# A two-layer decoder trunk on one core: PE queue order at the entry and the transition, and a later place for each chunk's finish

## The chip, the cores and the metric

The kernel runs on one NeuronCore of one Trainium2 chip. The core has five engines with queues of their own: PE (TensorE, matrix products), DVE (VectorE), ACT (ScalarE), POOL (GpSimd) and SP (SyncE, which here issues all transfers). Each engine works through its queue in the order in which the program was laid down, and waits at an instruction until its inputs are there. The metric is the device time of one execution in microseconds.

## What is computed

A decoder trunk on one sequence of 1024 tokens with 1024 channels, in float32: a short-convolution layer (A), then an attention layer (B) with 16 heads, then a root-mean-square norm.

```
# layer A
h = rmsnorm(x, g) * (1 + scale) + shift          # shift, scale, gate from silu(c) @ w + b
b_gate, c_gate, u, z = split(h @ w_in, 4)
y = b_gate * causal_dwconv(c_gate * u, conv_w) * silu(z)
x = x + gate * (y @ w_out)
# layer B
k, v = split(modulated_norm(x) @ w_kv, 2);  q, z = split(modulated_norm(x) @ w_qz, 2)
per 128-query block: s = q k^T / 8;  lb = log_sigmoid(s);  l1 = where(mask, lb - s, 0)
suffix = reversed_cumsum(l1) - l1;  a = where(mask, exp(lb + suffix), 0);  o = a v
x = x + gate * ((o * silu(z)) @ w_out)
out = rmsnorm(x, final_g)
```

## The kernel before, in words

All activations are kept transposed: 128 channels on the partitions, tokens along the columns, so a 1024x1024 activation is eight tiles of 128x1024. Every float32 operand of a product is split into a high part and a remainder (`xh`/`xl`, `whi`/`wlo`), and a product is three matmuls: high by high, high by rest, rest by high. The function `linear` (L181) does that for one output tile: 8 channel tiles times 3 matmuls, 24 in all, into one PSUM bank of 512 tokens (a "half"; NH is 2). A PSUM bank is named by its tag: `ps_mm`, `ps_z`, `ps_tr` and `ps_o`, two banks each; `ps_any` hands out the first three in turn.

The order on the engines is set by a scheduler that takes the instructions in program order as priority, fills gaps with later work by its own timing estimate, and obeys two extra means: `tc.high_priority()` and `tc.issue_after(i)`, which keeps the instructions of a block on the engine of `i` behind `i`.

The norms are all made the same way. The squares of eight channel tiles are summed into one tile; PE sums it over the partitions (`column_totals`, L105, or transposes and a reduction, L91 and L92); DVE makes 1/sqrt of the few numbers in twelve small steps (`rms_columns`, L202 to L209, the result is `ry`); PE spreads `ry` over all partitions by transposes (`row_block`, L215); and the result is multiplied into the tiles.

Entry of layer A (L305 to L324): the first tiles of the four projections of layer A (M_B, M_C, M_U, M_Z) are multiplied with the raw, not yet normalised `xh`/`xl` by `lin`, while the modulation vectors and the norm are still on their way. `spread = last["pe"]` is the last transpose that spreads the norm.

Transition (L430 to L475, L566 to L573): the output projection of layer A gives x1 half by half, eight tiles `s` each. For a half, L448 to L453 make the scale, L455 scales the eight tiles on DVE, L456 and L457 split them into `x1h` and `x1l`. Three weight tiles of layer B (`firsts`: a key, a query and a value tile) are prepared early; each has a vector `terms` whose sum over channels is the bias of its projection. `with_bias` (L493) makes that bias when it is first used: `shift_bias` (L174) transposes `terms` on PE (L177) into `ps_mm` and reduces it on DVE (L178). Then `project_qkv(0)` makes keys, queries and values of pair 0 for both halves; ACT and DVE add the bias as they read the bank (L521, L522).

The end (L766 to L778): the last output projection runs over three chunks of tokens, 512, 256 and 256 wide. For each chunk the tiles j = 4 to 7 are multiplied (24 matmuls each; tiles 0 to 3 were done before), then squared. A chunk's `finish` (L750) makes its norm and multiplies its eight tiles, six on POOL and two on DVE (L754), and stores each; `finish_last` (L757) does that for the last chunk on DVE alone, reading the scale from PSUM (L763).

Of the kernel before, what the change touches and what calls it, by code (L numbers as in the profile page):

```python
# [11 lines left out]
AF = mybir.ActivationFunctionType  # L12
ALU = mybir.AluOpType
AX = mybir.AxisListType.X

P = 128
# [10 lines left out]
EARLY = 4  # L27
# [3 lines left out]
CHUNKS = ((0, 512), (512, 768), (768, 1024))  # L31
# [6 lines left out]
def decoder_kernel(ctx, tc, vecs, xT, a_mod, kv_mod, b_mod, w_in, w_out_a, w_kv, w_qz, w_out_b, outT):  # L38
    nc = tc.nc
# [10 lines left out]
    last = {}  # L50
# [120 lines left out]
                acc, raw[:, kt * P:(kt + 1) * P], shift[:, kt:kt + 1], acc, op0=ALU.mult, op1=ALU.add)  # L171
        return acc

    def shift_bias(acc, tag):  # L174
        bias = const.tile([P, 1], F32, name="bias", tag="bias", bufs=8)
        ps = ps_tile(tag)
        nc.tensor.transpose(ps[:, :P], acc, ident)  # L177
        nc.vector.tensor_reduce(bias, ps[:, :P], AX, ALU.add)  # L178
        return bias

    def linear(ps, w, ah, al, sl, kts=range(KT)):  # L181
        hi, lo = w
        for kt in kts:
            wh, wl = hi[:, kt * P:(kt + 1) * P], lo[:, kt * P:(kt + 1) * P]
            nc.tensor.matmul(ps, lhsT=wh, rhs=ah[kt][:, sl], start=(kt == kts[0]), stop=False)  # L185
            nc.tensor.matmul(ps, lhsT=wh, rhs=al[kt][:, sl], start=False, stop=False)  # L186
            nc.tensor.matmul(ps, lhsT=wl, rhs=ah[kt][:, sl], start=False, stop=(kt == kts[-1]))  # L187


    def rms_columns(ssq, lo_t=0, hi_t=T, more=None, total=None):  # L190
# [36 lines left out]
    def halves():  # L227
        return [slice(h * HALF, (h + 1) * HALF) for h in range(NH)]
# [13 lines left out]
    M_B, M_C, M_U, M_Z = 0, 1, 2, 3  # L242
# [59 lines left out]
            split(hi_b, lo_b, raw_b, nc.gpsimd)  # L302
            first[M_B] = raw_b, hi_b, lo_b

    def lin(w):  # L305
        out = []
        for sl in halves():
            ps = ps_any()
            linear(ps, w, xh, xl, sl)
            out.append(ps)  # L310
        return out

# [8 lines left out]
        rms_rows(y_a, rbc_a)  # L321
    spread = last["pe"]

    first[M_B] = first[M_B][0], lin(first[M_B][1:])  # L324


    def modulated(x, gain, rms, shift, hi, lo):
# [104 lines left out]
    for sl in halves():  # L432
        ssq1 = tmp.tile([P, HALF], F32, name="ssq1", tag="graw", bufs=3)
        xs = []
        for j in range(KT):
            w = load_weights(w_out_a[j])[1:]
            xr = stile()
            xs.append(xr)
            nc.sync.dma_start(xr, xT[j * P:(j + 1) * P, sl])
            ps = ps_any()  # L440
            linear(ps, w, yh, yl, sl)
            nc.vector.scalar_tensor_tensor(xr, ps, mods["gate_a"][:, j:j + 1], xr, op0=ALU.mult, op1=ALU.add)
            nc.sync.dma_start(x1_dram[j, :, sl], xr)
            if j == 0:
                nc.scalar.activation(ssq1, xr, AF.Square)
            else:
                sq = tmp.tile([P, HALF], F32, name="sq1", tag="graw", bufs=3)
                nc.scalar.activation(sq, xr, AF.Square)  # L448
                if j < KT - 1:
                    nc.vector.tensor_add(ssq1, ssq1, sq)  # L450
        with tc.high_priority():

            scale = row_block(rms_columns(ssq1, 0, HALF, sq), 0, 4)  # L453
            for kt, x in enumerate(xs):
                nc.vector.tensor_mul(x, x, scale)  # L455
                nc.scalar.activation(x1h[kt][:, sl], x, AF.Copy)  # L456
                last["x1"] = nc.vector.tensor_tensor(x1l[kt][:, sl], x, x1h[kt][:, sl].bitcast(F32), op=ALU.subtract)  # L457
        if sl.start == 0:

            def first_raw(raw, w, m):  # L460
                nc.sync.dma_start(raw, w)
                return raw, scaled(raw, mods["gain_" + m], mods["shift_" + m])

            firsts = [
                first_raw(tmp.tile([P, D], F32, name="raw1", tag="gacc", bufs=1), w_kv[0], "kv"),
                first_raw(tmp.tile([P, 2 + T], F32, name="raw1", tag="v", bufs=2)[:, :T], w_qz[0], "b"),
                first_raw(raw_tile(), w_kv[NPAIR], "kv")]

    def parts(raw, pool=wpool, tags=("whi", "wlo"), bufs=2):
        hi, lo = (pool.tile([P, KT * P], F32R, name=n, tag=t, bufs=bufs) for n, t in zip(("whi", "wlo"), tags))  # L470
        split(hi, lo, raw, nc.gpsimd)
        return hi, lo

    first_w = [parts(raw) for raw, _ in firsts[:2]]
    papw.close()  # L475

# [17 lines left out]
    def with_bias(w, terms):  # L494
        bias = []

        def late():

            if not bias:
                bias.append(shift_bias(terms, "mm"))  # L500
            return bias[0]
        return w, late

    def projected(w, sl, ps_get=lambda: ps_tile("mm")):
        ps = ps_get()
        linear(ps, w, x1h, x1l, sl)
        return ps
# [4 lines left out]
    def project_qkv(p):  # L512
# [26 lines left out]
        def queries(sl, t, bias):  # L539
            ql = att.tile([P, HALF], F32, name="ql", tag="pt", bufs=2).bitcast(F32R)  # L540
            evacuate(t, bias, qq[0][:, sl], ql)
            move(qq[1][B, sl], qq[0][B, sl])
            move(qq[1][A, sl], ql[B])
            move(qq[0][B, sl], ql[A])
# [21 lines left out]

        if p == 0:
            first_w.append(parts(firsts[2][0], att, ("vv", "vv"), 4))
            (kw, kb), (qw, qb), (vw, vb) = (with_bias(w, terms) for w, (_, terms) in zip(first_w, firsts))
            for sl in halves():  # L570
                keys(sl, projected(kw, sl, ps_any), kb)
                queries(sl, projected(qw, sl, ps_any), qb)
                values(sl, projected(vw, sl, ps_any), vb)  # L573
        else:
            kw, kb = prepared(w_kv[p], mods["gain_kv"], mods["shift_kv"])
            for sl in halves():
                keys(sl, projected(kw, sl), kb)
            qw, qb = prepared(w_qz[p], mods["gain_b"], mods["shift_b"])
            for sl in halves():
                queries(sl, projected(qw, sl), qb)  # L580
            vw, vb = prepared(w_kv[NPAIR + p], mods["gain_kv"], mods["shift_kv"])
            for sl in halves():
                values(sl, projected(vw, sl), vb)
# [113 lines left out]
    def add_out(x2, j, sl, w, kts):  # L697
        ps = ps_any()[:, :sl.stop - sl.start]
        linear(ps, w, oh, ol, sl, kts)
        nc.vector.scalar_tensor_tensor(x2[:, sl], ps, mods["gate_b"][:, j:j + 1], x2[:, sl], op0=ALU.mult, op1=ALU.add)  # L700
# [66 lines left out]
    for c, (a, b) in enumerate(CHUNKS):  # L767
        sl = slice(a, b)
        for j in range(EARLY, KT):
            if c == 0:  # L770
                ws[j] = load_weights(w_out_b[j], None, "vv", "vv", att, 4)[1:] if j >= KT - 2 else load_weights(w_out_b[j])[1:]
                x2.append(residual(j))
            add_out(x2[j], j, sl, ws[j], range(KT))
            sq = squares(j, sl, c == len(CHUNKS) - 1 and j == KT - 1)
        if c < len(CHUNKS) - 1:
            finish(sl)
        else:
            finish_last(sl, sq)  # L778


# [39 lines left out]
```

## Time and profile before

| | before |
|---|---|
| time, median of 3 runs | 1195.78 us (1192.18 to 1450.73) |
| the profiled execution, time | 1193.45 us |
| its span | 1191.6 us |
| PE busy | 1160.2 us, 97% of the span, 6004 matmuls |
| DVE, ACT, POOL busy | 857.4, 457.6, 351.7 us |
| mean granted TensorE clock | 0.982 of full |
| transfers | 138.47 MB, mean 116 GB/s |

A busy share is an average over stages that have different limits. Matmuls are pipelined: the time from one start to the next is what each costs, and the duration shown is longer. The granted clock has two levels, 1.00 (2.4 GHz) and 0.50 (1.2 GHz).

### The profile page before, as it was taken

The page shows a single profiled execution, that of the slowest core. Times are in us where ns is not written, and L with a number is a line of the kernel's source. Part 1 is how long each engine was busy: PE and PEld are TensorE (multiplying, and loading weights), DVE is VectorE, ACT ScalarE, POOL GpSimd, SP SyncE. Part 2 cuts the span into 40 slices and gives each one's busy share as a digit, 9 for nine tenths or more (in the row PEclk, how much of TensorE's full clock was granted, in tenths as well). Part 3 has the DMA queues.
Part 4 walks back from the last instruction along what each step waited for, and adds up shares of the span by engine and source line. Part 5 has one row for each costly group of instructions (what it writes and reads, how often), then busy time and mean ns, then how long its engine had stood idle before and what let it go on. Part 6 is the DMA issues. An engine that isn't in the chain of part 4 may idle for free.

```text
span 1191.6 us, 15883 instructions
## 1 busy us (share of the span) xinstructions
PE 1160.2 (97%) x6004; PEld 987.6 (83%) x6004; DVE 857.4 (72%) x1271; ACT 457.6 (38%) x750; POOL 351.7 (30%) x205
## 2 busy tenths in 40 slices
PE   7999999999999999989999999999999999999995
PEld 6888888888888888868888888888888888887885
DVE  7679325446546487478898898888988888686466
ACT  4344211212212224234544545444545444454341
POOL 3014423433433453321231322303123032121424
PEclk9799999999999999989999999999999999999997
DMA  9534315345354544342313223132241323562204
GB/s 373 220 123 144 104 54 165 109 151 176 99 167 150 193 141 154 114 100 70 86 65 89 63 78 99 64 85 67 63 107 53 84 67 79 143 248 88 71 1 141
DMA packets 61436, 138.47 MB, mean 116 GB/s; under 512 B 7472, under 2 KB 11696, under 8 KB 61360
## 3 DMA queue, kind: packets, MB, share of 16 engines
q1 hardware_dynamic: 61360, 137.46, 36.5%
q8 instruction: 47, 0.77, 0.3%
q14 instruction: 29, 0.24, 0.1%
HBM read 103.87 MB, written 14.68 MB: 99 GB/s over the span
## 4 chain that ended last, share of the span: by engine, by line
PE 86%; DVE 10%; issue 2%; ACT 1%; DMA 0%; DVEq 0%; SPq 0%; ACTq 0%
PE ps_mm L185 12%; PE ps_mm L186 12%; PE ps_mm L187 12%; PE ps_z L186 5%; PE ps_z L187 5%; PE ps_z L185 5%; PE ps_tr L186 5%; PE ps_tr L187 5%; PE ps_tr L185 5%; PE ps_tr L628 4%; DVE sfx L618 3%; PE ps_o L643 3%; PE ps_o L642 2%; PE ps_z L610 2%; PE ps_z L609 2%
## 5 line engine op out<-in xcount | busy, mean ns | idle before, releaser
L144 POOL TENSOR_TENSOR wlo<-raw,whi 128x1024 fp32r<-128x1024 f32 x87 | 219.4, 2523 | 632.9 <-ACT whi L143 516.2
L618 DVE TENSOR_TENSOR_SCAN sfx<-sfx,floor 128x128 f32<-128x128 f32 (+2 forms) x192 | 226.0, 1197 | 18.2 <-ACT sfx L614 18.2
L185 PE MATMUL ps_mm<-x1h,whi 128*128 128x512 f32 x480 | 191.7, 399 | 4.1 <-DVE bias L178 4.1
L186 PE MATMUL ps_mm<-x1l,whi 128*128 128x512 f32 x480 | 190.1, 396 | 0.0
L187 PE MATMUL ps_mm<-x1h,wlo 128*128 128x512 f32 x480 | 188.8, 393 | 0.0
L143 ACT ACTIVATE whi<-raw 128x1024 fp32r<-128x1024 f32 x87 | 92.1, 1059 | 144.1 <-issue 39.6
L631 ACT ACTIVATE ah<-ps_tr,minus 128x512 fp32r<-128x512 f32 (+1 forms) x160 | 100.4, 646 | 109.5 <-PE ps_tr L628 107.9
L632 DVE SCALAR_TENSOR_TENSOR al<-ps_tr,ah 128x512 fp32r<-128x512 f32 (+1 forms) x160 | 97.6, 623 | 41.7 <-ACT ah L631 41.2
L614 ACT ACTIVATE sfx<-ps_z 128x128 f32<-128x128 f32 (+2 forms) x192 | 90.4, 492 | 77.9 <-PE ps_z L610 76.2
L185 PEld LDWEIGHTS ps_mm<-x1h,whi 128*128 128x128 f32 x480 | 90.6, 189 | 22.2 <-DVE bias L178 5.1
L187 PEld LDWEIGHTS ps_mm<-x1h,wlo 128*128 128x128 f32 x480 | 90.6, 189 | 17.7
L121 DVE SCALAR_TENSOR_TENSOR gacc<-graw,cs,gacc 128x512 f32<-128x512 f32 x84 | 72.5, 885 | 44.9 <-DMA graw<-b_mod 22.1
L186 PEld LDWEIGHTS ps_mm<-x1l,whi 128*128 128x128 f32 x480 | 90.6, 189 | 16.6 <-DVE x1l L457 0.3
L628 PE MATMUL ps_tr<-ident,sfx 128*128 128x128 f32 x576 | 88.1, 274 | 0.0
L643 PE MATMUL ps_o<-al,vv 128*128 128x256 f32 x320 | 82.7, 294 | 4.3 <-DVE al L632 4.3
L642 PE MATMUL ps_o<-ah,vv 128*128 128x256 f32 x320 | 86.4, 282 | 0.1
L643 PEld LDWEIGHTS ps_o<-al,vv 128*128 128x128 f32 x320 | 60.4, 189 | 11.7 <-DVE al L632 8.7
L609 PE MATMUL ps_z<-kh,qq 128*128 128x128 f32 (+1 forms) x192 | 68.9, 364 | 0.7 <-ACT sfx L614 0.7
L642 PEld LDWEIGHTS ps_o<-ah,vv 128*128 128x128 f32 x320 | 60.5, 189 | 7.3 <-ACT ah L631 0.6
L628 PEld LDWEIGHTS ps_tr<-ident,sfx 128*128 128x128 f32 x576 | 65.5, 141 | 1.0
L610 PE MATMUL ps_z<-kl,qq 128*128 128x128 f32 (+1 forms) x192 | 65.3, 349 | 0.0
L185 PE MATMUL ps_mm<-nh,whi 128*128 128x512 f32 x152 | 59.4, 391 | 0.0
(277 smaller groups left out, 2435.0 us busy)
## 6 DMA issues: line engine op xcount, KB each, us to landing
raw<-w_in SPq DMA_DIRECT2D x29, 512.0 KB, 4.2
graw<-b_mod SPq DMA_DIRECT2D x48, 256.0 KB, 3.1
stage<-a_mod SPq DMA_DIRECT2D x16, 512.0 KB, 9.8
s<-xT SPq DMA_DIRECT2D x32, 256.0 KB, 4.8
graw<-kv_mod SPq DMA_DIRECT2D x32, 256.0 KB, 3.4
raw<-w_qz SPq DMA_DIRECT2D x16, 512.0 KB, 3.9
raw<-w_out_a SPq DMA_DIRECT2D x16, 512.0 KB, 3.5
raw<-w_kv SPq DMA_DIRECT2D x16, 512.0 KB, 3.6
```

Of the source, the lines that this page charges most:

```text
L143: nc.scalar.activation(hi, full, AF.Copy)
L144: lo_eng.tensor_tensor(lo, full, hi.bitcast(F32), op=ALU.subtract)
L185: nc.tensor.matmul(ps, lhsT=wh, rhs=ah[kt][:, sl], start=(kt == kts[0]), stop=False)
L186: nc.tensor.matmul(ps, lhsT=wh, rhs=al[kt][:, sl], start=False, stop=False)
L187: nc.tensor.matmul(ps, lhsT=wl, rhs=ah[kt][:, sl], start=False, stop=(kt == kts[-1]))
L609: nc.tensor.matmul(zps[:, :w], lhsT=qq[:, qs], rhs=kh[:, c0:c0 + w], start=True, stop=False)
L618: nc.vector.tensor_tensor_scan(rev, rev, floor[:, z0:z0 + w][:, ::-1], sf[r][:, s0 + w:s0 + w + 1], op0=ALU.mult, op1=ALU.max)
L628: nc.tensor.transpose(tp[:, s * P:(s + 1) * P], rows[r][:, jb * P - c0:(jb + 1) * P - c0], ident)
L631: nc.scalar.activation(ah[:, :w], tp[:, :w], AF.Identity, bias=minus)
L632: nc.vector.scalar_tensor_tensor(al[:, :w], tp[:, :w], -1.0, ah[:, :w].bitcast(F32), op0=ALU.add, op1=ALU.subtract)
L642: nc.tensor.matmul(ops[:, cols], lhsT=vs, rhs=ah[:, rs], start=first, stop=False)
L643: nc.tensor.matmul(ops[:, cols], lhsT=vs, rhs=al[:, rs], start=False, stop=end)
```

## The change

In the entry, the second half of M_B's first product is put behind `spread` on PE. In the transition, the three biases of `firsts` are made ahead of `project_qkv`, with high priority, behind the last matmul of layer A's output projection (`out_last`): PE transposes into `ps_tr`, and ACT reads the bank with a copy that also writes the sum of each row (L179 of the change). The queries of pair 0 are put behind the last transpose of `row_block`. At the end, a chunk's `finish` is written behind the first two tiles of the next chunk.

```
-    def shift_bias(acc, tag):
+    def shift_bias(acc, tag, eng=nc.vector):
         bias = const.tile([P, 1], F32, name="bias", tag="bias", bufs=8)
         ps = ps_tile(tag)
         nc.tensor.transpose(ps[:, :P], acc, ident)
-        nc.vector.tensor_reduce(bias, ps[:, :P], AX, ALU.add)
+        if eng is nc.scalar:
+            nc.scalar.activation(acc, ps[:, :P], AF.Copy, accum_out=bias)
+        else:
+            nc.vector.tensor_reduce(bias, ps[:, :P], AX, ALU.add)
         return bias
...
-            nc.tensor.matmul(ps, lhsT=wl, rhs=ah[kt][:, sl], start=False, stop=(kt == kts[-1]))
+            last["mm"] = nc.tensor.matmul(ps, lhsT=wl, rhs=ah[kt][:, sl], start=False, stop=(kt == kts[-1]))
...
-    def lin(w):
+    def lin(w, behind=None):
         out = []
-        for sl in halves():
+        for h, sl in enumerate(halves()):
             ps = ps_any()
-            linear(ps, w, xh, xl, sl)
+            if behind is not None and h:
+
+                with tc.issue_after(behind.ins):
+                    linear(ps, w, xh, xl, sl)
+            else:
+                linear(ps, w, xh, xl, sl)
             out.append(ps)
         return out
...
-    first[M_B] = first[M_B][0], lin(first[M_B][1:])
+    first[M_B] = first[M_B][0], lin(first[M_B][1:], spread)
...
+        out_last = last["mm"]
         with tc.high_priority():
 
             scale = row_block(rms_columns(ssq1, 0, HALF, sq), 0, 4)
...
+    with tc.high_priority(), tc.issue_after(out_last.ins):
+        first_b = [shift_bias(terms, "tr", nc.scalar) for _, terms in firsts]
     first_w = [parts(raw) for raw, _ in firsts[:2]]
     papw.close()
...
             first_w.append(parts(firsts[2][0], att, ("vv", "vv"), 4))
-            (kw, kb), (qw, qb), (vw, vb) = (with_bias(w, terms) for w, (_, terms) in zip(first_w, firsts))
+            (kw, kb), (qw, qb), (vw, vb) = ((w, lambda b=b: b) for w, b in zip(first_w, first_b))
             for sl in halves():
                 keys(sl, projected(kw, sl, ps_any), kb)
-                queries(sl, projected(qw, sl, ps_any), qb)
+
+                with tc.issue_after(last["pe"].ins):
+                    q = projected(qw, sl, ps_any)
+                queries(sl, q, qb)
                 values(sl, projected(vw, sl, ps_any), vb)
...
             add_out(x2[j], j, sl, ws[j], range(KT))
+            if j == EARLY + 1 and c > 0:
+
+                finish(slice(*CHUNKS[c - 1]))
             sq = squares(j, sl, c == len(CHUNKS) - 1 and j == KT - 1)
-        if c < len(CHUNKS) - 1:
-            finish(sl)
-        else:
-            finish_last(sl, sq)
+    finish_last(sl, sq)
```

The change's lines stand a few numbers higher: L215 of before is L218, L455 and L457 are L464 and L466, L185 to L187 are L188 to L190, L754 is L768.

PE's queue in the transition, before, from the last query matmul of the first half (into `ps_z`) to the first matmuls of the second half:

```order
L187 MATMUL ps_z<-x1h,wlo 128x512
L177 MATMUL ps_mm<-ident,bacc 128x128
L215 MATMUL ps_o<-ident,ry 128x128 x4
L177 MATMUL ps_mm<-ident,bacc 128x128
L185 MATMUL ps_z<-x1h,whi 128x512
L185 MATMUL ps_mm<-x1h,whi 128x512
L186 MATMUL ps_mm<-x1l,whi 128x512
```

The same place in the change, from the last bias product on; the keys of the first half go into `ps_mm`, the queries into `ps_z`:

```order
L177 MATMUL ps_tr<-ident,bacc 128x128
L188 MATMUL ps_mm<-x1h,whi 128x512
L189 MATMUL ps_mm<-x1l,whi 128x512
L105 MATMUL ps_o<-one,sq_3703 128x1 x4
L190 MATMUL ps_mm<-x1h,wlo 128x512
L188 MATMUL ps_mm<-x1h,whi 128x512
L189 MATMUL ps_mm<-x1l,whi 128x512
L190 MATMUL ps_mm<-x1h,wlo 128x512
L218 MATMUL ps_o<-ident,ry 128x128 x4
L188 MATMUL ps_z<-x1h,whi 128x512
```

The broadcast of `ry` has moved from behind the 24 query matmuls to ahead of them, and the bias products to ahead of L105.

DVE's queue at the same place, before, from the last two steps of `ry`:

```order
L208 SCALAR_TENSOR_TENSOR rt<-rt,rv 128x4
L209 SCALAR_TENSOR_TENSOR ry<-rt,ry 128x4
L178 TENSOR_REDUCE bias<-ps_mm 128x1
L455 TENSOR_TENSOR s<-s,ps_o 128x512 x8
L178 TENSOR_REDUCE bias<-ps_mm 128x1
L457 TENSOR_TENSOR x1l<-s,x1h 128x512 x8
```

and in the change:

```order
L211 SCALAR_TENSOR_TENSOR rt<-rt,rv 128x4
L212 SCALAR_TENSOR_TENSOR ry<-rt,ry 128x4
L464 TENSOR_TENSOR s<-s,ps_o 128x512 x8
L466 TENSOR_TENSOR x1l<-s,x1h 128x512 x8
L168 TENSOR_SCALAR bacc<-raw,shift_b 128x128
```

The reductions of the biases have left DVE's queue; on ACT the sum of the first stands ahead of the last square, the other two behind it.

PE's queue at the end, before, inside the last tile of the last chunk (`ps_mm`); the first L215 belongs to the `finish` of the middle chunk, the last to `finish_last`:

```order
L186 MATMUL ps_mm<-ol,whi 128x256
L215 MATMUL ps_o<-ident,ry 128x128 x2
L187 MATMUL ps_mm<-oh,wlo 128x256
L185 MATMUL ps_mm<-oh,whi 128x256
L186 MATMUL ps_mm<-ol,whi 128x256
...
L105 MATMUL ps_o<-one,ssq_9870 128x1 x2
L105 MATMUL ps_o<-one,sq_10434 128x1 x2
L215 MATMUL ps_o<-ident,ry 128x128 x2
```

and in the change:

```order
L189 MATMUL ps_mm<-ol,whi 128x256
L190 MATMUL ps_mm<-oh,wlo 128x256
L218 MATMUL ps_o<-ident,ry 128x128 x2
L105 MATMUL ps_o<-one,ssq_9870 128x1 x2
L105 MATMUL ps_o<-one,sq_10434 128x1 x2
L218 MATMUL ps_o<-ident,ry 128x128 x2
```

The middle chunk's broadcast has moved behind the last matmul of the program.

## Rows read from the trace of the kernel before

**Rows 1.** The head of the page.

```profile
span 1191.6 us, 15883 instructions
```

**Rows 2.** Busy time by stretch: stretch, length, each engine, PEclk, DMA share, GB/s.

```profile
20.00:507.00 487.00, 487.00 (x2253) 407.43 (x2252) 280.39 (x396) 132.03 (x174) 168.77 (x81) 0.98 0.44 147
519.00:1173.90 654.90, 648.81 (x3649) 560.56 (x3648) 542.74 (x809) 307.80 (x549) 168.72 (x104) 1.00 0.30 87
```

**Rows 3.** PE's waits: what waited, for what: total us, times, longest.

```profile
PE ps_o L215 <- DVE ry L209: 5.7, 2, 3.3
PE ps_o L643 <- DVE al L632: 4.3, 8, 0.7
PE ps_mm L185 <- DVE bias L178: 4.1, 3, 3.2
```

**Rows 4.** Timeline of PE, transition: start, length, instruction, idle before and its releaser.

```profile
500.18 0.94 PE L105 MATMUL ps_o<-one,sq 128*128 128x1 f32 x8
...
501.55 0.40 PE L185 MATMUL ps_z<-x1h,whi 128*128 128x512 f32 x1
...
507.03 0.27 PE L177 MATMUL ps_mm<-ident,bacc 128*128 128x128 f32 x1
507.14 0.60 PE L215 MATMUL ps_o<-ident,ry 128*128 128x128 f32 x4
507.69 0.33 PE L177 MATMUL ps_mm<-ident,bacc 128*128 128x128 f32 x1
509.18 0.50 PE L185 MATMUL ps_z<-x1h,whi 128*128 128x512 f32 x1 [1.17 <-ACT x1h L456]
512.90 0.80 PE L185 MATMUL ps_mm<-x1h,whi 128*128 128x512 f32 x1 [3.22 <-DVE bias L178]
...
518.63 0.39 PE L186 MATMUL ps_mm<-x1l,whi 128*128 128x512 f32 x1
```

**Rows 5.** Timeline of ACT and DVE, transition.

```profile
495.19 0.63 ACT L448 ACTIVATE sq<-s 128x512 f32<-128x512 f32 x1
...
503.35 0.16 DVE L209 SCALAR_TENSOR_TENSOR ry<-rt,ry 128x4 f32<-128x4 f32 x1
...
507.78 1.88 DVE L455 TENSOR_TENSOR s<-s,ps_o 128x512 f32<-128x512 f32 x3
...
512.57 0.28 DVE L178 TENSOR_REDUCE bias<-ps_mm 128x1 f32<-128x128 f32 x1
512.77 7.12 DVE L457 TENSOR_TENSOR x1l<-s,x1h 128x512 fp32r<-128x512 f32 x8
```

**Rows 6.** Busy time by stretch, behind the transition's waits.

```profile
515.00:517.00 2.00, 2.00 (x6) 1.60 (x5) 2.00 (x3) 0.41 (x1) 1.60 (x1) 0.50 0.46 100
```

**Rows 7.** One-column products in layer A's entry, and the clock around them.

```profile
85.10 1.84 PE L363 MATMUL ps_o<-shift_a,stage 128*128 128x1 f32 x16
85.00:87.00 2.00, 2.00 (x19) 1.96 (x18) 2.00 (x4) 0.78 (x2) 0.00 (x0) 1.00 0.64 200
```

**Rows 8.** The end: PE's timeline, and a stretch behind the first wait.

```profile
1176.58 0.40 PE L215 MATMUL ps_o<-ident,ry 128*128 128x128 f32 x2 [2.40 <-DVE ry L209]
1184.64 0.66 PE L215 MATMUL ps_o<-ident,ry 128*128 128x128 f32 x2 [3.33 <-DVE ry L209]
1177.20:1178.00 0.80, 0.80 (x7) 0.80 (x5) 0.69 (x2) 0.59 (x2) 0.00 (x0) 0.51 0.00 0
```

**Rows 9.** The end: timeline of POOL and DVE.

```profile
1165.71 8.75 POOL L754 TENSOR_TENSOR x<-x,rbc 128x512 f32<-128x512 f32 x6 [26.64 <-DVE rbc L222]
1169.48 1.26 DVE L204 TENSOR_SCALAR rt<-rv 128x2 int32<-128x2 int32 x1
...
1176.28 0.16 DVE L209 SCALAR_TENSOR_TENSOR ry<-rt,ry 128x2 f32<-128x2 f32 x1
1178.15 4.56 POOL L754 TENSOR_TENSOR x<-x,rbc 128x256 f32<-128x256 f32 x6 [3.69 <-DVE rbc L222]
1182.09 0.65 DVE L205 TENSOR_SCALAR ry<-rt 128x2 int32<-128x2 int32 x1
```

## Prediction, made before the changed kernel ran

> **What bounds the kernel now.** I read the head of the page first. The profiled execution has a span of 1191.6 us [rows 1] and a time of 1193.45 us, so 1.85 us lie around the span; it stands between the median of the three runs (1195.78) and the lowest (1192.18), and every sum below starts from 1193.45. Next I asked for PE's busy time in two long stretches: from 20 to 507 us it is busy for all 487.00 us, and from 519 to 1173.9 us for 648.81 of 654.90 [rows 2]. What an edit does inside those stretches is therefore paid only if it adds or removes PE work, or opens a gap. What is left are two places, and the list of PE's waits names them: 4.1 us for `bias`, most of it in one piece in the transition into layer B, and 5.7 us for `ry`, at the end [rows 3]. The timelines of these two places carry the rest.
>
> **The transition, PE now.** The scale of layer A's second half is made in this way: sums over partitions on PE (L105), twelve small DVE steps to `ry` (L202 to L209), a transposing broadcast on PE (L215), then DVE scales eight tiles (L455), and ACT and DVE split them (L456, L457). `ry` is ready at 503.35 + 0.16 = 503.51 [rows 5], but L215 starts only at 507.14 [rows 4]: it stands in PE's queue behind 24 query matmuls, from 501.55 to 507.03, 0.228 us each [rows 4]. Then PE has little ready: it waits 1.17 us for `x1h` and 3.22 us for a bias whose reduction (L178) stands on DVE behind the eight scalings [rows 4, 5]. And after that the clock is low: it reads 0.50 (1.2 GHz) from 515 to 517 [rows 6], and the first matmul in full pace again starts at 518.63 [rows 4]. So from 507.03 to 518.63, 11.60 us, PE does two L177 (0.11 each), one L215 (507.14 to 507.69, 0.55) and 14 matmuls (3.19): 3.96 us of work. **The transition loses 7.6 us.**
>
> **The transition, changed.** Three edits act on it. The queries are put behind L215, so the broadcast stands four matmuls after L105, with the 24 of the queries behind it. The three bias products stand earlier, and their sums move from DVE to ACT. So DVE has nothing between the last step of `ry` and the eight scalings. Step by step: ahead of L105 there are two matmuls less (0.46) and two L177 more (0.22), so L105 starts at 500.18 - 0.24 = 499.94. From its start to `ry` took 3.33 us (500.18 to 503.51), and from the end of `ry` to a waiting L215 0.14 (1176.28 + 0.16 to 1176.58) [rows 4, 5, 8, 9], so the broadcast starts at 503.4. PE comes to it after L105 (0.81) and 4 matmuls (with the gap behind L105 1.0), at 501.75. **A wait of 1.7 us is added**, with all 24 query matmuls and everything else of PE behind it. Then: the broadcast until 503.95, the 24 matmuls until 509.45. DVE starts scaling 0.64 us after the broadcast starts (507.14 to 507.78), at 504.05, needs 4.8 us for eight (507.78 to 512.57), ends at 508.85, and has the first `x1l` about 0.8 us later, 509.65 [rows 4, 5]. PE wants it at its third matmul of the second half, 509.9, and then one per six matmuls (1.37 us) against 0.89 per tile (eight in 7.12 [rows 5]): no second wait, with 0.25 us to spare at the start. Gain: 7.6 - 1.7 = **5.9 us**.
>
> The price of a sum on ACT is not in the trace, which has no activation with an accumulated sum. From below it is the 0.28 us that the same reduction takes on DVE, from above the 0.63 us of an ACT pass over four times as many columns [rows 5], doubled for a second pass; I take 0.3 to 0.6, since the operand is the small one. One of the three stands ahead of the square `sq` in ACT's queue, which ran at 495.19, while the L105 that reads it ran at 500.18 [rows 4, 5]: even 1.26 would be hidden. The other two follow the square and lie before `x1h`, with ACT idle there.
>
> **The entry, cost nothing.** Putting the second half of M_B behind the broadcast takes four matmuls out of PE's early queue, and four of M_B's first half come up: the broadcast has as many matmuls ahead of it as before. PE has no gap there to fill or to lose [rows 2]. If the work that moved up were late, four matmuls would cost 0.9 us; if the tiles came earlier, PE could not use it. I take 0.
>
> **The end, now.** `finish` of the middle chunk has its broadcast (L215) inside the last tile, behind 17 of its 24 matmuls. Its `ry` is late, at 1176.28 + 0.16 = 1176.44, and PE waits 2.40 us with seven matmuls behind [rows 8, 9]. It is late because POOL multiplies the first chunk from 1165.71 for 8.75 us, and beside it four DVE steps on 128x2 numbers take some 1.26 us each, against 0.16 later [rows 9]. In the last reduction the same happens on a smaller scale: beside POOL's six 256-column multiplies (4.56 us from 1178.15) a step takes 0.65 us [rows 9].
>
> **The end, changed.** The first chunk's broadcast stays where it was in PE's queue (11 matmuls into the last chunk), so POOL's long stretch stays until 1174.5. The middle chunk's sums come 18 matmuls later, after two tiles of the last chunk, and its broadcast after the last matmul: PE's 2.40 us wait is gone and its matmuls end at about 1175.0. But DVE begins the twelve steps some 1.8 us later, still beside POOL; about four are through when POOL ends at 1174.5, and the other eight at 0.2 and two larger operations (0.9 together) give `ry` at 1177.0, not 1176.44. So POOL's second stretch starts where it did, near 1178.1, and ends near 1182.7. The last reduction can start at about 1179.5, some 2 us earlier, because the last `x` no longer comes late, but it runs beside POOL: four or five steps at 0.65 until 1182.7, then seven at 0.2, so that the last broadcast starts at 1184.2 against 1184.64 [rows 8]. **The end gains 0.4 us**, not 2.4: it is now bound by POOL's multiplies. What follows, the last eight multiplies and the stores, is unchanged.
>
> **The sum.** 1193.45 - 5.9 - 0 - 0.4 = 1187.15, say **1187.2 us**. From the third of the eight head pairs on, every engine's order is that of before; in pairs 0 and 1 the order changes, and gaps there can go or come in sizes like the waits for `al` now, 0.5 to 0.7 us each [rows 3], so plus or minus 1.
>
> **Rivals.** (a) The clock falls in the new wait. For it: after the 2.40 us wait at the end the clock read 0.51 within a microsecond of the resumption [rows 8], and here 0.81 us of one-column products lies four matmuls ahead of the wait. Against it: after 1.84 us of one-column products at 85.10 it stayed at 1.00 [rows 7]. The old low stretch cost 518.63 - 512.90 = 5.73 us for 13 matmuls, 2.8 more than in full pace [rows 4]; the new wait is under half as long as the old ones, so I take half, 1.4: 1188.6. (b) On the other side, the wait only changes place: the new 1.7 us comes on top of a later wait for `x1l`. My margin there is 0.25 us; if the split of the eight tiles starts 3.2 us later than I put it, that wait and its low clock come back whole, 1.7 + 3.2 + 2.8 = 7.7, no gain; with (a)'s 1.4 on top 1194.6, slower than before. It decides from a first `x1l` at 513 on. Against it stands that DVE's queue has nothing between `ry` and the scalings. (c) The end passes all of PE's 2.40 us on, because POOL's multiplies start earlier than I put them: 1185.2. (d) POOL holds the last reduction up altogether: its eleven steps run only after 1182.7, 2.2 us, and the broadcast starts at 1185.0, so the end loses 0.4 instead: 1188.0. The Trainium skill ("SBUF — State Buffer", section "Who interferes with whom") has the rule for this: a VectorE instruction with two SBUF inputs and a GpSimd one that reads SBUF exclude each other, and the later one fully blocks. By that rule the end would come out as in (d). The trace agrees that such steps are slowed, but they did advance beside POOL, at 0.65 us in the one stretch and 1.26 in the other [rows 9].
>
> **How the numbers follow.** Chances: the forecast 0.50, (a) 0.22, (b) 0.06, (c) 0.12, (d) 0.10. The forecast's own range, with pairs 0 and 1 at plus or minus 1 and the runs' spread of 1.3 below and 2.3 above 1193.45, is 1185 to 1190.5. The whole range goes from (c) less the pairs and the spread, 1183, to (b), 1194.5. 2% of the time is 24 us, about what a measurement of this kernel tells from no change, and the largest thing in reach here is 7.6 + 2.4 us. So within 2%: 0.97; faster by more 0.02; slower by more 0.01.
>
> **What would show it.** Right: PE's waits have no entry for `bias` at the transition and one of about 1.7 us for `ry` ahead of the broadcast, the first scaling starts about 3.7 us earlier against L105, and the clock reads 1.00 from there to the end of the queries. At the end no wait inside the last tile, some of the twelve middle steps at 1.2 us, and the last reduction starting some 2 us earlier with several steps at 0.65. Wrong: a second wait for `x1l` behind the queries, a stretch of 0.50 after the new wait, new waits over 1 us in pairs 0 and 1, or a wait before 507 us.

## The result, and the profile after

The changed kernel took 1188.54 us in the median of eleven runs (1179.74 to 1191.09), the kernel before 1195.51 in eleven. The medians are 7.0 us apart. One run of the kernel before was slow, at 1450.73 us, and the ratio goes by the others: it is 0.9934, with a 95% interval of 0.9916 to 0.9952. That is 7.9 us less, against 6.3 forecast from the profiled execution (8.3 against the median before). The time lies within 2% of the kernel before, and inside the range. The profiled execution took 1184.95 us; the medians of other kernels below go with their own interval. Where a kernel has one run, its time says little, since the runs of one kernel lie some 11 us apart, and it is read by its trace.

| | before | after |
|---|---|---|
| span of the profiled execution | 1191.6 | 1183.2 us |
| PE busy | 1160.2 | 1154.1 us |
| mean granted clock, profiled execution | 0.982 | 0.988 |
| L105 of the transition starts | 500.18 | 498.48 us |
| from it to the first scores of layer B (L609, L623) | 31.69 | 26.34 us |
| from it to the last attention product (L643, L657) | 605.80 | 599.81 us |
| first chunk's scale copied (L222, L225) to the last eight multiplies | 20.40 | 19.58 us |

The two profiles differ by 8.4 us, and the landmarks divide them: 1.70 before L105, 5.35 in the transition, 0.64 in head pairs 0 and 1, and 0.82 at the end (together 8.51; 0.05 went back before the end's copy, 0.06 behind its multiplies). The landmarks of the transition and of the end, before and then after:

```profile
531.87 0.22 PE L609 MATMUL ps_z<-kh,qq 128*128 128x128 f32 x1
1164.94 0.69 DVE L222 COPY rbc<-ps_o 128x512 f32<-128x512 f32 x1 [0.35 <-PE ps_o L215]
1185.34 2.74 DVE L763 TENSOR_TENSOR out<-x,ps_o 128x256 f32<-128x256 f32 x8 [0.85 <-PE ps_o L215]
```

```profile
524.82 0.30 PE L623 MATMUL ps_z<-kh,qq 128*128 128x128 f32 x1
1157.30 0.69 DVE L225 COPY rbc<-ps_o 128x512 f32<-128x512 f32 x1 [0.35 <-PE ps_o L218]
1176.88 2.74 DVE L777 TENSOR_TENSOR out<-x,ps_o 128x256 f32<-128x256 f32 x8 [0.84 <-PE ps_o L218]
```

The first scores have another place in PE's queue. From L105 on they stand behind 102 wide matmuls (512 columns) in the change and behind 98 before, and behind one bias transpose fewer: at 0.228 and 0.11 us each, 0.80 us more work. At equal work the transition therefore gives 6.15 us. Pairs 0 and 1, which have two wide matmuls and one transpose less to do, give about 0.1 and not 0.64.

PE's waits after, which answer to [rows 3] (what waited, for what: total us, times, longest):

```profile
PE ps_o L218 <- DVE ry L212: 8.8, 3, 5.5
PE ps_o L657 <- DVE al L646: 4.3, 8, 0.7
PE ps_mm L188 <- DVE bias L181: 0.4, 1, 0.4
```

The wait of 3.2 us for a bias is gone, and so is the one for `x1h`. The waits for `ry` have grown from 5.7 to 8.8 us: one is new in the transition, one has moved behind the last matmul, and the last one is longer.

The transition on PE, which answers to [rows 4]:

```profile
498.48 0.95 PE L105 MATMUL ps_o<-one,sq 128*128 128x1 f32 x8
...
501.95 0.62 PE L218 MATMUL ps_o<-ident,ry 128*128 128x128 f32 x4 [1.49 <-DVE ry L212]
...
507.89 0.39 PE L188 MATMUL ps_mm<-x1h,whi 128*128 128x512 f32 x1
508.12 0.40 PE L188 MATMUL ps_z<-x1h,whi 128*128 128x512 f32 x1
508.36 0.39 PE L189 MATMUL ps_mm<-x1l,whi 128*128 128x512 f32 x1
```

On ACT and DVE, which answers to [rows 5]; two of the three sums on ACT are shown:

```profile
497.87 0.28 ACT L179 ACTIVATE bacc<-ps_tr 128x128 f32<-128x128 f32 x1 [3.36 <-PE ps_tr L177]
498.04 0.19 ACT L179 ACTIVATION_READ_ACCUMULATOR bacc<-ps_tr 128x1 f32 x1
498.21 0.28 ACT L179 ACTIVATE bacc<-ps_tr 128x128 f32<-128x128 f32 x1
...
501.64 0.16 DVE L212 SCALAR_TENSOR_TENSOR ry<-rt,ry 128x4 f32<-128x4 f32 x1
502.61 4.87 DVE L464 TENSOR_TENSOR s<-s,ps_o 128x512 f32<-128x512 f32 x8 [0.81 <-PE ps_o L218]
507.39 7.16 DVE L466 TENSOR_TENSOR x1l<-s,x1h 128x512 fp32r<-128x512 f32 x8
```

The broadcast starts 3.47 us after L105, in place of 6.96, and PE runs without a gap from it into the second half. Behind it the clock stays up, in the stretch that answers to [rows 6] (stretch, length, each engine, PEclk, DMA share, GB/s):

```profile
509.00:517.00 8.00, 8.00 (x36) 6.58 (x36) 8.00 (x20) 1.25 (x3) 2.77 (x1) 1.00 0.16 35
```

The end on PE, which answers to [rows 8]:

```profile
1169.35 0.40 PE L218 MATMUL ps_o<-ident,ry 128*128 128x128 f32 x2 [1.79 <-DVE ry L212]
1176.18 0.66 PE L218 MATMUL ps_o<-ident,ry 128*128 128x128 f32 x2 [5.48 <-DVE ry L212]
```

POOL and DVE there, which answers to [rows 9]:

```profile
1158.07 8.95 POOL L768 TENSOR_TENSOR x<-x,rbc 128x512 f32<-128x512 f32 x6 [26.69 <-DVE rbc L225]
1170.29 4.55 POOL L768 TENSOR_TENSOR x<-x,rbc 128x256 f32<-128x256 f32 x6 [3.27 <-DVE rbc L225]
1163.29 1.25 DVE L207 TENSOR_SCALAR rt<-rv 128x2 int32<-128x2 int32 x1
...
1172.17 0.65 DVE L208 TENSOR_SCALAR ry<-rt 128x2 int32<-128x2 int32 x1
...
1174.89 0.16 DVE L210 TENSOR_TENSOR rt<-ry 128x2 f32<-128x2 f32 x1
```

The wait of 2.40 us inside the last tile has become one of 1.79 us behind it. The last reduction starts 2.25 us earlier against the copy of the first chunk's scale, but its next five steps (0.50 to 0.65 us) run beside POOL's second stretch, and the last broadcast is won only 0.82 us. The middle chunk's own reduction still has three steps of 1.2 us beside POOL's first stretch (four before).

### The profile page after: what moved, and what is told of

Same layout as the page of the kernel before. It is cut to its first block, busy times and chain, and to the rows that moved or that the text cites. A ratio compares the mean times of both kernels' runs of the same rounds, so it can differ in the third digit from the quotient of the medians.

```text
span 1183.2 us, 15886 instructions
## 1 busy us (share of the span) xinstructions
PE 1154.1 (98%) x6004; PEld 982.8 (83%) x6004; DVE 864.2 (73%) x1268; ACT 458.8 (39%) x756; POOL 353.5 (30%) x205
## 4 chain that ended last, share of the span: by engine, by line
PE 86%; DVE 11%; issue 2%; ACT 1%; DMA 0%; DVEq 0%; SPq 0%
PE ps_mm L188 12%; PE ps_mm L190 12%; PE ps_mm L189 12%; PE ps_z L189 5%; PE ps_z L190 5%; PE ps_z L188 5%; PE ps_tr L189 5%; PE ps_tr L190 5%; PE ps_tr L188 5%; PE ps_tr L642 4%; DVE sfx L632 3%; PE ps_o L657 3%; PE ps_o L656 2%; PE ps_z L624 2%; PE ps_z L623 2%
## 5 line engine op out<-in xcount | busy, mean ns | idle before, releaser
L188 PE MATMUL ps_mm<-x1h,whi 128*128 128x512 f32 x480 | 190.9, 398 | 0.4 <-DVE bias L181 0.4
L190 PE MATMUL ps_mm<-x1h,wlo 128*128 128x512 f32 x480 | 188.3, 392 | 0.0
L188 PEld LDWEIGHTS ps_mm<-x1h,whi 128*128 128x128 f32 x480 | 90.2, 188 | 18.2 <-DVE bias L181 1.1
L190 PEld LDWEIGHTS ps_mm<-x1h,wlo 128*128 128x128 f32 x480 | 90.3, 188 | 17.5
L657 PE MATMUL ps_o<-al,vv 128*128 128x256 f32 x320 | 82.7, 294 | 4.4 <-DVE al L646 4.3
L657 PEld LDWEIGHTS ps_o<-al,vv 128*128 128x128 f32 x320 | 60.4, 189 | 12.0 <-DVE al L646 8.8
L623 PE MATMUL ps_z<-kh,qq 128*128 128x128 f32 (+1 forms) x192 | 69.2, 366 | 0.7 <-ACT sfx L628 0.7
L188 PE MATMUL ps_mm<-nh,whi 128*128 128x512 f32 x152 | 59.4, 391 | 0.0
```

The source lines that it names most:

```text
L190: last["mm"] = nc.tensor.matmul(ps, lhsT=wl, rhs=ah[kt][:, sl], start=False, stop=(kt == kts[-1]))
L623: nc.tensor.matmul(zps[:, :w], lhsT=qq[:, qs], rhs=kh[:, c0:c0 + w], start=True, stop=False)
L657: nc.tensor.matmul(ops[:, cols], lhsT=vs, rhs=al[:, rs], start=False, stop=end)
```

## The experiments

### Which of the edits brings the gain

The parts of the change can be applied one by one. The entry's edit alone (`lin(first[M_B][1:], spread)` and the `behind` in `lin`):

> Only the entry's edit (the second half of M_B's first product behind the spread), all else as before. Theory A (the four matmuls that change places are full-pace work either way): 0 +- 1 us against the kernel before, ratio 1.000; runs of both kernels spread by several us with the granted clock of layer A's entry, and the two spreads overlap. Rival R1 (the edit itself keeps the clock up in the entry, which would explain that the changed kernel reached its transition 1.7 us earlier than before): 1.5 to 3 us faster, ratio 0.9975 or less, with a higher mean clock than the kernel before in most runs.

Measured: 1194.82 us, ratio 0.9995 (0.9976 to 1.0014). L105 started at 503.11, not earlier than before. The edit brings nothing that the runs can tell, and rival R1 falls.

The transition's edits alone (early biases and queries behind the broadcast):

> Only the transition's edits (early biases on ACT, queries behind the broadcast). Theory A: the transition holds nearly the whole gain, -5.9 us, ratio 0.995; PE waits about 1.5 us ahead of the broadcast and not at all for x1h or the biases, and no stretch of 0.50 follows. Rival R1 (a quarter of the gain belongs to the entry) leaves the same here; rival R2 (the edits need one another, since the entry's change also moves the scheduler's estimate for what follows): under 4 us.

Measured: 1190.19 us, ratio 0.9947 (0.9921 to 0.9972), 6.3 us. PE waits 1.49 us for `ry` ahead of the broadcast, as in the whole change, and no stretch of 0.50 follows. From L105 to the first scores it takes 26.35 us, as in the whole change, so rival R2 falls. Nearly all of the gain is here.

The later finish alone (the last hunk of the diff):

> Only the finish of each chunk moved behind two tiles of the next. Theory A (the end is bound by POOL's multiplies, which slow DVE's small steps): 0.4 to 0.9 us faster, too little for the interval, but to be read from the last stretch of the trace: from the copy of the first chunk's scale on DVE to the start of the last eight multiplies 20.40 us before, 19.6 to 20.0 here. Rival R3 (the whole wait of 2.40 us inside the last tile is won): 18.0 us.

Measured: 1194.64 us, ratio 1.0001 (0.9981 to 1.0020), so its effect is too small for the runs. The trace shows it: 19.56 us from the copy of the first chunk's scale to the last multiplies. All the profiles here repeat it: 20.38 to 20.40 us in the five kernels with the old finish, 19.56 to 19.58 in the six with the new one and POOL in both chunks. So 0.82 us, as theory A had it, and R3 falls.

The change without its entry edit:

> The change without its entry edit. Theory A: as the whole change, ratio 0.993 to 0.995, -6.3 us plus or minus the clock of the entry. Rival R1: 1.5 to 3 us slower than the whole change, ratio 0.995 to 0.996, with the mean clock of its runs below that of the whole change (median 0.985 over eleven runs).

Measured: 1185.12 us in six runs, ratio 0.9915 (0.9886 to 0.9945). It is not slower than the whole change; that it looks faster is within the two intervals. R1 falls here too.

### Which half of the transition

The biases early, the queries where they were (entry and end are as before too; the lines are marked against the change):

```
-                with tc.issue_after(last["pe"].ins):
-                    q = projected(qw, sl, ps_any)
-                queries(sl, q, qb)
+                queries(sl, projected(qw, sl, ps_any), qb)
```

> One half of the transition's edits: the three biases early on ACT, but the queries ahead of the broadcast as before. Theory A (the gain comes from the broadcast that no longer stands behind 24 query matmuls; the biases only remove DVE's one reduction of 0.28 us): PE still reaches the broadcast 7 us after L105, then waits about 1.2 us for x1h and 3 to 4 us for x1l in place of the bias, with a stretch of 0.50 behind it; gain of the transition 0 to 1 us. Rival R4 (the bias was the cause, as the name of the longest wait before says): the wait of 3.22 us and its low clock are gone, gain 3.2 to 6 us.

One run: 1198.20 us, beside 1197.16 for the kernel before. PE's timeline in the transition:

```profile
511.85 0.60 PE L218 MATMUL ps_o<-ident,ry 128*128 128x128 f32 x4
513.89 0.50 PE L188 MATMUL ps_mm<-x1h,whi 128*128 128x512 f32 x1 [1.44 <-ACT x1h L460]
...
518.02 0.80 PE L189 MATMUL ps_mm<-x1l,whi 128*128 128x512 f32 x1 [3.39 <-DVE x1l L461]
```

The stretch behind it (columns as in [rows 2], the clock third from the end):

```profile
517.00:523.00 6.00, 4.98 (x12) 3.92 (x13) 6.00 (x7) 3.12 (x5) 2.73 (x1) 0.51 0.20 44
```

The wait that the profile of before put down to the bias is there in full, for `x1l`: 3.39 us. From L105 to the first scores it took 32.27 us, against 31.69 before. The bias was only the last name on a wait whose cause was the late scale; R4 falls.

The queries behind the broadcast, the biases late and on DVE as before, and nothing else changed:

> The other half: the queries behind the broadcast, the biases made late and on DVE as before. Theory A: the broadcast starts 3.5 to 5 us after L105 (three reductions of 0.28 us stand among the steps of ry), PE waits 2 to 3.5 us there and under 1 us later; gain of the transition 3.5 to 5 us. Rival R4: the wait for a bias stays behind the queries, gain under 2 us.

One run: 1193.08 us. PE's timeline:

```profile
503.95 0.33 PE L177 MATMUL ps_mm<-ident,bacc 128*128 128x128 f32 x1 [0.38 <-DVE bias L178]
505.80 1.09 PE L215 MATMUL ps_o<-ident,ry 128*128 128x128 f32 x4 [1.52 <-DVE ry L209]
```

The stretch behind it:

```profile
506.00:511.00 5.00, 5.00 (x15) 4.03 (x15) 4.07 (x7) 3.35 (x6) 0.00 (x0) 0.50 0.01 2
```

The broadcast starts 3.87 us after L105, PE's waits are down to 1.90 us, and still only 2.46 us are won to the first scores (29.23). The rest is the clock. It fell to 0.50 in this wait: twelve query matmuls take 5.22 us in place of 2.74 (0.228 each), and the broadcast 0.74 in place of 0.37, some 2.9 us together; with them the gain would be 5.3. This is rival (a) of the prediction, in a kernel next to the changed one. Theory A had 3.5 to 5 and missed this; R4 falls, since no long wait for a bias is left. So in these traces the two halves of the transition need each other: alone they give -0.6 and 2.46 us, together 5.35 (at equal work -0.3, 2.7 and 6.15). With the biases out of the way there is no wait of 0.38 us ahead of the long one, `ry` comes 0.40 us sooner after L105, and the clock stays at 1.00 through a wait of nearly the same length. It does so in all six profiles that have this wait of 1.49 us. That it falls with late biases is one execution; whether it falls in others is not shown.

### What bounds the transition now

Six of the 24 query matmuls ahead of the broadcast, into the new wait:

```
...
+                q = ps_any()
+                linear(q, qw, x1h, x1l, sl, range(2), True, False)
                 with tc.issue_after(last["pe"].ins):
-                    q = projected(qw, sl, ps_any)
+                    linear(q, qw, x1h, x1l, sl, range(2, KT), False)
```

> The change with the first 6 of each half's 24 query matmuls ahead of the broadcast, so that PE has 1.37 us of work in its new wait of 1.49 us. Theory D (behind the broadcast DVE's eight scalings and the first x1l set when PE goes on; PE had 0.25 us to spare): the wait for ry falls below 0.2 us, a wait of 1.1 to 1.4 us for x1l appears behind the queries, and from L105 to the first matmuls of the second half that read x1l nothing is won (0 to 0.3 us). Rival R5 (PE's own work is the bound): 1.3 us won, no wait for x1l over 0.3.

One run: 1184.48 us.

```profile
501.58 0.62 PE L218 MATMUL ps_o<-ident,ry 128*128 128x128 f32 x4
...
506.17 0.39 PE L188 MATMUL ps_mm<-x1h,whi 128*128 128x512 f32 x1
...
507.77 0.50 PE L189 MATMUL ps_mm<-x1l,whi 128*128 128x512 f32 x1 [0.98 <-DVE x1l L466]
```

The wait for `ry` is filled, and one of 0.98 us for `x1l` comes in its place. From L105 (498.11) to the first matmul that reads the new `x1l` it takes 9.66 us, against 9.88. Theory D holds and R5 falls: 0.22 us won of 1.37. This is also the margin on which rival (b) of the prediction hung: the step from `ry` to the first `x1l` had about 0.2 us to spare.

The same with DVE taking turns, one tile scaled, the one before split (each scaling behind the splitting two tiles before):

```
...
+                with ExitStack() as behind:
+                    if sl.start > 0 and kt > 1:
+                        behind.enter_context(tc.issue_after(subs[kt - 2].ins))
+                    nc.vector.tensor_mul(x, x, scale)
...
```

> As with the six query matmuls ahead of the broadcast, and besides DVE takes turns between scaling a tile and splitting the one before, in place of eight scalings first. Theory D (with the wait for ry filled, the first x1l sets when PE goes on): the first x1l is there 2.5 us earlier, the wait of 0.98 us for x1l is gone and no other of over 0.3 us comes, and the third matmul of the second half starts 8.6 to 8.9 us after L105, against 9.88 in the change and 9.66 with the filling alone. Rival R9 (ACT and DVE waiting on each other in turns make a later x1l late): waits of together 1 us or more in the second half.

One run: 1191.94 us. The matmul that reads the first `x1l` starts at 513.23, 8.50 us after L105 (504.73): the place has won 1.38 us, as theory D says, and no wait for `x1l` is left, so R9 falls. But it does not last. To the first scores 0.71 us are left of it (25.63 against 26.34), and from L105 to the last attention product it takes 600.50 us, 0.69 more than in the change. The order of pairs 0 and 1 is another, and PE waits nine times for `al`, 5.1 us, in place of eight times and 4.3. The kernel with the transition's edits alone has the same nine waits (5.2 us) and 600.71 us; the change without its entry edit has eight and 599.76. So what the scheduler does with the two pairs behind is worth some 0.9 us either way, about as much as the last step here.

### The end: POOL and DVE

The middle chunk's eight multiplies on DVE, which reads the scale from PSUM:

```
+        if sl.start > 0:
+            scale = row_block(rms_columns(ssq2, sl.start, sl.stop), 0, (sl.stop - sl.start) // P)
+            for j in range(KT):
+                nc.vector.tensor_tensor(x2[j][:, sl], x2[j][:, sl], scale, op=ALU.mult)
+                nc.sync.dma_start(outT[j * P:(j + 1) * P, sl], x2[j][:, sl])
+            return
```

> The change with the middle chunk's eight multiplies all on DVE, reading the scale from PSUM; POOL has none of them. Theory P (POOL's multiplies slow DVE's small steps in the last reduction, five at 0.50 to 0.65 us in the changed kernel): the last reduction starts about 1.1 us later, since DVE has 2.74 us of multiplies first, but all its twelve steps take 0.16, and the last broadcast starts 0.9 to 1.2 us earlier; from the copy of the first chunk's scale to the last eight multiplies 18.4 to 18.7 us against 19.58. Rival R6 (the long steps belong to these instructions in this place, not to POOL): 20.3 to 20.8 us.

One run: 1190.18 us. DVE at the end:

```profile
1176.25 2.74 DVE L768 TENSOR_TENSOR x<-x,ps_o 128x256 f32<-128x256 f32 x8 [0.19 <-PE ps_o L218]
1178.90 0.15 DVE L205 TENSOR_SCALAR rv<-ps_o 128x2 f32<-128x2 f32 x1
1179.09 0.17 DVE L207 TENSOR_SCALAR rt<-rv 128x2 int32<-128x2 int32 x1
1179.30 0.17 DVE L208 TENSOR_SCALAR ry<-rt 128x2 int32<-128x2 int32 x1
```

The same steps take 0.17 us with POOL idle, against 0.50 and 0.65, and from the copy of the first chunk's scale to the last multiplies it takes 18.30 us, against 19.58: 1.28 us won, although DVE does 2.74 us of multiplies ahead of the steps. Theory P holds, R6 falls. In the change, POOL's six 256-column multiplies take 4.55 us, 0.76 each, and a step beside them 0.65; the 512-column ones take 8.95, 1.49 each, and a step beside those 1.2. One step gets through for each multiply: in the second stretch POOL's start at 1172.08, 1172.76 and 1173.44, DVE's steps at 1172.17, 1172.85 and 1173.53. The Trainium skill ("SBUF — State Buffer", section "Who interferes with whom") has it, for a VectorE instruction in a two-port mode, that whichever of VectorE and GpSimd issues first gets the shared pair of ports for its whole instruction, while the other is fully blocked. The steps look like that if "whole instruction" is taken at its word: one multiply, not the row of six. No run here shows in which mode they run. Rival (d) of the prediction had the steps held up for the whole row, and it did not come. Nor is every DVE instruction held: an addition of 128x256 in POOL's first stretch took 0.41 us, against 0.43 without POOL.

Both chunks in this way (`if sl.stop < T:`), so that POOL has nothing at the end:

> The change with both finishes' multiplies on DVE, reading the scale from PSUM; POOL has none. Theory P (POOL's first stretch, 8.95 us, stretches three of the middle chunk's steps to 1.2 us each, and so makes its ry late): all steps take 0.16, PE waits under 0.8 us for the middle chunk's ry against 1.79, and from the broadcast of the first chunk's scale to the last eight multiplies 16.5 to 17.5 us against 20.2 (1156.66 to 1176.88). Rival R8 (DVE's added multiplies, some 1.8 and 1.0 us, eat up what the steps win): 18.9 to 20 us, no better than POOL off the middle chunk alone (18.9 by the same landmarks).

One run: 1185.51 us. PE's broadcasts:

```profile
1159.53 0.60 PE L218 MATMUL ps_o<-ident,ry 128*128 128x128 f32 x4
...
1171.16 0.40 PE L218 MATMUL ps_o<-ident,ry 128*128 128x128 f32 x2 [0.74 <-DVE ry L212]
...
1176.73 0.66 PE L218 MATMUL ps_o<-ident,ry 128*128 128x128 f32 x2 [4.38 <-DVE ry L212]
```

No step is over 0.17 us, and the middle chunk's `ry` keeps PE for 0.74 us in place of 1.79. From the first broadcast to the last eight multiplies (1177.43) it takes 17.90 us, against 20.22 in the change and 21.04 before. The mechanism is theory P's, but the size is between the two expectations, 16.5 to 17.5 and 18.9 to 20, and R8 falls: DVE's own row is now the bound, 2.74 us of multiplies and 2.3 of steps between the last products and the last broadcast.

### The spread of the runs

The eleven runs of the change lie 11 us apart, and their mean clocks, 0.981 to 0.993, order them almost perfectly (correlation -0.993): 1179.74 us at 0.993, 1191.09 at 0.982. The rows of the clock on the page (tenths, 40 slices) show where in the profiled executions it is lost, first before, then after, then the kernel of the next experiment:

```profile
PEclk9799999999999999989999999999999999999997
```

```profile
PEclk8899999999999999999999999999999999999998
```

```profile
PEclk9999999999999999999999999999999999999997
```

Before, there are two places ahead of the end: layer A's entry (first four slices) and the transition (the 8). After, the entry alone. How much the entry costs can be added up from 20 to 180 us in steps of 1 us, counting half of the time at 0.50: 10.24 us before, 8.53 after. L105 of the transition less this cost stands at 489.94 and 489.95 us, and between 489.2 and 490.0 in all twelve profiles without the edit of the next experiment, while L105 itself lies between 493.20 and 504.94. So the low clock of the entry accounts for when the transition starts, and for all of the 1.70 us.

In the entry PE does 64 one-column products in one row (L293 before, L296 after), and in the stretch that begins with them the clock reads 0.61 before and 0.81 after, with the same instructions in the same number. To test it, the last four groups of these products were put behind the halves of the two first products of `lin`, and without high priority:

```
     for m in (M_C, M_U):
-        pss = lin(first[m][1:])
+        pss = lin(first[m][1:], then=(4, 5) if m == M_C else (6, 7))
...
             out.append(ps)
+            if then[h] is not None:
+                totals(then[h])
```

> The change with layer A's last four groups of one-column products set apart: the 64 that PE did in one row in the entry now stand in groups of at most 16 between wide matmuls (counted as the trace counts them). Theory C (the spread of the runs, 1179.7 to 1191.1, is the low clock of layer A's entry, and the low clock follows the row of 64): the stretch of 0.50 behind it, 6.8 to 13.7 us long in the profiles so far, is gone or half as long, the mean clock of the runs rises by 0.003 to 0.006 over the changed kernel's 0.986, the time falls by 3 to 7 us below its 1188.5, and the runs spread less. Rival R7 (the clock there falls for other reasons): mean clock 0.984 to 0.987 and ratio to the kernel before 0.993 as the change.

Measured: 1182.13 us in six runs (1179.72 to 1184.35), ratio 0.9901 (0.9874 to 0.9928), mean clock of the runs 0.9915 against 0.9862 of the change's. The stretches that begin with these products, before, after and here (columns as in [rows 2]):

```profile
44.32:62.00 17.68, 17.68 (x83) 16.16 (x82) 8.29 (x17) 2.04 (x3) 0.31 (x1) 0.61 0.08 29
```

```profile
47.62:65.30 17.68, 17.68 (x102) 16.07 (x101) 9.96 (x21) 2.75 (x4) 2.40 (x1) 0.81 0.00 1
```

```profile
45.70:63.40 17.70, 17.70 (x115) 15.64 (x113) 9.91 (x15) 4.28 (x6) 5.35 (x2) 1.00 0.02 6
```

In the same time PE gets through 83, 102 and 115 instructions. Theory C holds and R7 falls, with the price of a new wait of 1.29 us for `ry` in the entry. The row of 64 is not the only place: the entry also has rows of 32 such products, and during or behind the first of them the clock falls to 0.50 in twelve of the fourteen profiles, in the spaced kernel's too (about 28 to 35 us). Breaking up those rows was not tried. What decides how long the clock stays low from run to run with an unchanged order stays open: these runs show that it varies, not why.

All that helped, together:

> All that helped together: the change, one-column products set apart, six query matmuls ahead of the broadcast with DVE taking turns, and both finishes on DVE from PSUM. If the theories C, D and P hold: 3 to 7 us for the clock, 1.0 to 1.3 in the transition, 2.5 to 3.5 at the end, so 1177 to 1182 us, ratio to the kernel before 0.985 to 0.989. If C falls: 1183 to 1186.

Measured: 1180.39 us in six runs (1177.97 to 1184.61), ratio 0.9892 (0.9861 to 0.9922), faster than the kernel before; its interval touches that of the change (0.9916 to 0.9952) only at the edge. It is 1.7 us below the spaced kernel, which the intervals do not tell apart; in its trace the end takes 17.90 us from the first broadcast, as with both chunks on DVE, and the nine waits for `al` are there again.

## Why the prediction held, step by step

- **The transition's waits: right.** Put at: broadcast 3.46 us after L105 (3.47), wait for `ry` 1.7 (1.49), no wait behind, clock at 1.00. Its 5.9 us, the idle time and low clock that go away, stand against 6.15 at equal work (5.35 by the landmark); most of the difference is the wait, put 0.21 too long. The price of the ACT sum was taken as 0.3 to 0.6 us, and one follows the other after 0.34. The margin of 0.25 us for the first `x1l` was right too: filling the wait won 0.22.
- **What the prediction did not see there:** how near the other outcome lay. With late biases the clock fell in a wait of 1.52 us and took some 2.9 us; rival (a) had a chance of 0.22 and 1.4 us as its price. And part of the 5.35 hangs on the one execution of before: in the kernels with the later finish alone and with the entry's edit alone, whose transition is that of before, L105 to the first scores took 30.79 and 30.78 us and not 31.69, since the low clock behind the waits ended sooner. Against those the gain is 4.45, or 5.25 at equal work.
- **The entry: the edit at 0 was right, the profile's 1.70 us was not.** L105 came 1.70 us earlier and not 0.24. The entry's edit alone brings nothing that the runs can tell. The 1.70 us are the clock of the entry (10.24 us lost before, 8.53 after, as added up above), and the 0.24 of the reordering doesn't show beside it. That clock was in the range as the runs' spread, but the spread is wider than the three runs of before suggested: 29 runs of that kernel lay between 1187.0 and 1198.0.
- **The end: right in mechanism, 0.4 us put where 0.82 came.** The step that was mis-sized is the start of the last reduction: put 1.85 us earlier (1179.5 against 1181.35 in the trace before), it came 2.25 earlier, and these 0.40 us are nearly all of the difference. The middle chunk had three slow steps, not four. That the gain is not the 2.40 us of the wait was right, and why: without POOL beside them the same steps take 0.17.
- **Pairs 0 and 1:** 0.64 us less by the landmarks, about 0.1 at equal work, inside the 1 us allowed. In other kernels here the same two pairs cost 0.9 us more by a ninth wait for `al`.
- **The sum:** 5.35 + 0.64 + 0.82 are the work of the edits, 6.8 us, and 7.1 if the 0.24 ahead of L105 is counted; the rest of the 1.70, the entry's clock, is luck of the profiled execution. The forecast of 6.3 and the measured 7.9 (interval 5.7 to 10.0) both fit it.

## What to carry to other kernels

A wait is named after the operand that came last; before removing that operand's work, ask what stands ahead of the instruction that released it, here a broadcast behind 24 matmuls that nobody waited for. Two edits that each look like the cure can need each other, so measure both halves. Before a gain is read from a landmark, count the work ahead of it: here the first scores had moved behind four more matmuls, which hid 0.8 us. Small steps of DVE that set the end should not run beside a long row of POOL's multiplies, and PE's row of tiny products is worth breaking up with wide ones where the clock falls in it or behind it.

## What the runs showed of the hardware

- The run's time follows the mean granted clock: 0.011 more of it was 11 us less, at an unchanged order. Where PE did 64 one-column products in a row, the clock fell to 0.50 before the row was over in every profile that has such a row (twelve); where the same products stood in groups of 16 or fewer between wide matmuls it read 1.00 (both profiles that have them).
- The clock fell in a wait of 1.52 us with one of 0.38 shortly ahead of it (0.50 from 506 to 511 us, one execution), and did not in one of 1.49 us without (six profiles).
- DVE steps on 128x2 numbers take 0.16 us alone, 0.65 beside POOL's 256-column multiplies (0.76 each) and 1.2 beside its 512-column ones (1.49 each), one step to a multiply.
- An ACT copy of 128x128 with a sum shows as two records, 0.28 and 0.19 us, and the next starts 0.34 us after it.
